# Two transformer blocks on one core: weight blocks in flight, the first modulation set in quarters, and a new written order

## The chip, the cores and the metric

The kernel runs on one core of a Trainium2 chip. The core has a matrix engine (TensorE, PE in the profile, with its weight loads as PEld), a vector engine (VectorE, DVE), a scalar engine (ScalarE, ACT), GpSimd (POOL) and SyncE (SP), which here issues nearly all transfers. The metric is device time in microseconds of the whole launch.

## The reference, cut to what matters

Two blocks work on 256 token rows of 1024 numbers (x) and on 256 context rows.

- **First block.** `mod = silu(c) @ w_mod + b_mod` gives six vectors for x; the same matrix with `c_ctx` gives those of the context. `h = rmsnorm(x) * n1 * (1 + scale) + shift`, and the like for the context. A gated linear attention follows: q, k, v, r are products of h with slices of `gla_w_in`, the decay comes from a small gate product, and `y = (norm(o) * silu(r)) @ w_out`; `x = x + g1 * y`. Then a mixture of 16 experts: each row is given two experts out of one of four groups, `out += gate * (silu(h@w1) * (h@w3)) @ w2`, `x = x + g2 * out`, and a last rmsnorm with `final_g`.
- **Second block.** Two layers of attention (latent and grouped heads; then windowed heads with a short convolution) on x, with keys and values of a second context that is projected from inputs of its own and does not depend on the first block.

Everything is in 32-bit floating point. The weights are read from HBM once: some 222 MB.

## The kernel before, in words

**How work is recorded and ordered.** The program is first recorded: every call on an engine becomes an `Op` (its function is called at line 384, which is therefore the line of almost all rows). `Sched.emit` (line 504) then plays the ops through a list planner with a cost for each op, picks an order, and issues the instructions in it. Each engine runs its own instructions strictly in that order, and SyncE issues the transfers strictly in that order too. An op's place is pulled forward or back by a table `PRI`: a number for its section (`sch.sec`, such as `rc2`, `rank`, `moe3`, `Gq`) and one for its run of 24 ops in the section.

**Buffers.** A weight block is mostly 1 MB (128 partitions of 8 KB). Blocks, split copies of weights (`cv`), projected heads and gathered rows share one pool `b` of 17 buffers of 8 KB a partition. Of these at most `WC = 5` may be weight blocks at a time (`sch.subcap`), and at most `CC = 5` split copies. PSUM has 8 banks (`ps`). A transfer into a buffer is issued when the last reader of the buffer's old content is done; until then SyncE stands, and all transfers behind it.

**The start** (line 1510). x is normed by rows. `gemv_half(h)` makes half of the first modulation set: four weight blocks (`modh`), on each of which 32-column products in four column groups run, then a copy by ScalarE, two transposes and six small VectorE ops. After both halves, section GN transposes x, modulates it (`split_evac`: a high and a low part), and section GM does so for the context. `dense` then makes q (`gq`), r (`gr0`, `gr1`) and k, v; the order of these sections is written in `GLASEQ`.

**The experts.** Routing is sections `rt`, `rc1`, `rc2`; section `rank` sorts the experts by their number of rows, and `eid` gives the expert number of each rank. Rank 15 is always expert 0. A load for another rank (`loadr`, line 2055) reads its expert number from `eid` into a register of SyncE (row line 2065), and its transfer's address is worked out from it (line 2066). So the first such load waits for `eid`. Each expert has six 1 MB blocks. The projections and attention of the second context (`cth`) are woven into the experts' sections by `merge` as other work for TensorE.

**Behind the experts.** `overflow` (line 2216) is an ordered stop of all engines: each reads a count and skips a branch that is not taken here (its rows have line 2222). Then section `t2` norms the result (`facc`) twice, as sums of squares over rows of 1024, and `adaln_T` (line 1218) transposes it for the second block.

Of the kernel before, what the change touches and what calls it, by code (L numbers as in the profile page):

```python
# [93 lines left out]
def _chunks(i):  # L94
# [10 lines left out]
    m = _kt(mods[0])[:, :, :2048].reshape(128, 8, 2, 2, 512)  # L105
    for h in range(2):
        for k2 in range(4):
            out[f"modh{h}_{k2}"] = m[:, 2 * k2:2 * k2 + 2, :, h]
# [43 lines left out]
def host(i):  # L152
# [40 lines left out]
ALT = 1  # L193
# [12 lines left out]
PRI = {  # L206
# [2107 lines left out]
```

## Time and profile before

| | |
|---|---|
| median of 3 runs | 891.46 us (890.01 to 892.35) |
| the profiled execution | 890.18 us, span 888.4 us |
| TensorE busy | 844.4 us (95%) |
| VectorE, ScalarE busy | 578.3 us, 416.4 us |
| mean granted TensorE clock | 0.991 |
| bytes read | 222 MB, mean 251 GB/s |

Busy time is the union of the recorded instructions. A matmul's record holds its latency, so that gaps shorter than it do not show as idle. PEld is the weight load of the matrix engine and overlaps PE. In the tables by stage PEclk is the granted clock as a share of full speed, "DMA share" the mean busy share of the 16 DMA engines.

### The profile page before, as it was taken

Reading aid. Unit: us, or ns where it says so; the run is one execution under the profiler, and the core shown is the slowest. Engines: PE = TensorE matmul, PEld = TensorE weight load, DVE = VectorE, ACT = ScalarE, POOL = GpSimd, SP = SyncE. Lnnn points to the kernel's source line nnn. Section 1 sums busy time; section 2 is a strip of 40 time slices with the busy share of each in tenths; the row PEclk is TensorE's granted clock in tenths of the full one; section 3 lists DMA queues with packets and bytes.
Section 4 is the critical chain, followed back from the end, with each engine's and each line's share of the span. In section 5 each row is a group of like instructions: output and inputs, shape, how many; then the busy total and the mean of one; then the engine's idle time right before and its main releaser. Section 6 shows DMA issues by size and latency. Waiting matters only on the chain. (4 is left out here: it accounts for less than half of the span.)

```text
span 888.4 us, 15257 instructions
## 1 busy us (share of the span) xinstructions
PE 844.4 (95%) x5830; PEld 598.1 (67%) x5830; DVE 578.3 (65%) x1608; ACT 416.4 (47%) x819; POOL 0.9 (0%) x5
## 2 busy tenths in 40 slices
PE   4999999999999999999988995999999999999997
PEld 2677667767875656555633432688876778899986
DVE  2676889428984623444755424989866558899783
ACT  3466545226433222224444433555489715454890
POOL 0000000000000000000000000000000000000000
PEclk9999999999999999999999999899999999999999
DMA  9954961877526999999999998884713203465101
GB/s 381 415 217 181 377 252 58 303 327 285 189 100 229 416 357 374 342 386 371 360 416 373 403 420 317 315 355 143 281 52 142 96 1 142 167 248 204 49 1 48
DMA packets 32834, 224.14 MB, mean 252 GB/s; under 512 B 3568, under 2 KB 3824, under 8 KB 7408
## 3 DMA queue, kind: packets, MB, share of 16 engines
q1 hardware_dynamic: 32608, 222.56, 64.6%
q8 instruction: 48, 0.79, 0.3%
q0 software_dynamic: 144, 0.52, 0.2%
q14 instruction: 34, 0.28, 0.1%
HBM read 222.02 MB, written 1.05 MB: 251 GB/s over the span
## 5 line engine op out<-in xcount | busy, mean ns | idle before, releaser
L384 DVE TENSOR_TENSOR cv<-w,cv 128x1024 fp32r<-128x1024 f32 (+3 forms) x128 | 145.2, 1150 | 26.5 <-ACT cv L384 26.3
L384 ACT ACTIVATE cv<-w 128x1024 fp32r<-128x1024 f32 (+3 forms) x128 | 124.3, 998 | 57.6 <-DMA w<-in_w_dram 36.5
L384 PE MATMUL ps<-hh,cv 128*128 128x256 f32 x576 | 114.4, 288 | 0.2 <-ACT cv L384 0.2
L384 PEld LDWEIGHTS ps<-hh,cv 128*128 128x128 f32 x576 | 92.2, 191 | 5.9 <-issue 4.1
L384 PE MATMUL ps<-w,xg 128*32 128x512 f32 (+1 forms) x544 | 87.8, 605 | 3.3 <-DMA w<-in_w_dram 3.2
L384 PE MATMUL ps<-hl,cv 128*128 128x256 f32 x288 | 81.4, 285 | 0.0
L384 PE MATMUL ps<-cv,hh 128*128 128x512 f32 (+2 forms) x288 | 78.5, 352 | 0.4 <-ACT hh L384 0.4
L384 ACT ACTIVATE t<-ps 128x512 f32<-128x512 f32 (+5 forms) x77 | 36.0, 477 | 84.1 <-PE ps L384 67.4
L384 PE MATMUL ps<-c_col,t 128*128 128x128 f32 x384 | 63.0, 280 | 5.6 <-ACT t L384 4.9
L384 PEld LDWEIGHTS ps<-c_col,t 128*128 128x128 f32 x384 | 44.1, 141 | 33.8 <-ACT t L384 22.0
L384 ACT ACTIVATE t<-ps,s,f 128x512 f32<-128x512 f32 (+1 forms) x80 | 54.9, 690 | 18.6 <-DVE s L384 18.3
L384 PE MATMUL ps<-w,cs 128*32 128x512 f32 (+1 forms) x448 | 50.9, 563 | 12.8 <-DVE s L384 9.1
L384 PE MATMUL ps<-cv,mixh 128*128 128x512 f32 x192 | 60.7, 394 | 0.0
L384 DVE TENSOR_REDUCE s<-ps 128x1 f32<-128x512 f32 (+1 forms) x80 | 45.1, 580 | 20.3 <-PE ps L384 20.1
L384 PE MATMUL ps<-w,t 128*32 128x512 f32 (+1 forms) x320 | 54.2, 599 | 3.6 <-issue 3.0
L384 PEld LDWEIGHTS ps<-hl,cv 128*128 128x128 f32 x288 | 54.9, 191 | 2.8 <-issue 2.4
L384 PEld LDWEIGHTS ps<-cv,hh 128*128 128x128 f32 x288 | 49.7, 189 | 10.0 <-issue 2.4
L384 PEld LDWEIGHTS ps<-w,xg 128*32 128x32 f32 (+1 forms) x544 | 23.0, 118 | 47.1 <-issue 37.0
L384 PE MATMUL ps<-cv,hl 128*128 128x512 f32 (+2 forms) x144 | 49.0, 348 | 0.0
L384 ACT ACTIVATE PT<-ps 128x512 f32<-128x512 f32 (+1 forms) x80 | 39.3, 510 | 20.6 <-PE ps L384 20.3
L384 PE MATMUL ps<-cv,hlh 128*128 128x512 f32 x128 | 42.1, 403 | 0.0
L384 PEld LDWEIGHTS ps<-cv,mixh 128*128 128x128 f32 x192 | 35.7, 188 | 7.3 <-issue 0.4
(269 smaller groups left out, 1515.5 us busy)
## 6 DMA issues: line engine op xcount, KB each, us to landing
w<-in_w_dram SPq DMA_DIRECT2D x198, 1024.0 KB, 7.5
ctx<-in_ctx_dram SPq DMA_DIRECT2D x3, 1024.0 KB, 7.8
w<-in_w_dram SPq DMA_DIRECT2D x4, 576.0 KB, 8.3
x<-in_x_dram SPq DMA_DIRECT2D x2, 1024.0 KB, 7.2
w<-in_w_dram SPq DMA_DIRECT2D x4, 512.0 KB, 3.7
w<-in_w_dram SPq DMA_DIRECT2D x2, 768.0 KB, 9.5
out_dram<-x SPq DMA_DIRECT2D x2, 512.0 KB, 2.6
c_cst<-in_cst_dram SPq DMA_DIRECT2D x1, 528.0 KB, 14.8
```

Source lines behind the costliest of these rows:

```text
L384: op.fn = lambda: getattr(real, fn)(*a, **k)
```

## The change

- **Weight blocks:** `WC` is 7, not 5. The pool `b` stays at 17 buffers.
- **First modulation set:** in four quarters, not two halves. A quarter takes two 1 MB blocks, 128-column products, one transpose, two VectorE ops. Behind each quarter stand a half block each (512 KB) of `gq` and `gr0`, two of eight column steps of x's transposing and modulating, and the products of `gq` and `gr0` on these two steps. Their sums stay in four PSUM banks from the first quarter to the last.
- **Products on zeros:** 20 of 512 columns at the start (section `wu`), and two of 256 columns behind each step of the first quarter, into a PSUM bank that nobody reads.
- **Experts' numbers:** the ops that make `eid` stand in a section of their own right behind the positions, ahead of the first gathering, not in `rank` behind it.
- **Norm behind the experts:** the products with `final_g` and the sums of squares by halves of 512 columns, and one add.
- **Order:** the planner runs four times, each time on the order of the run before and with a table of its own (364, 1462, 1331 and 1000 entries, not one of 356). The tables also name runs of six ops and single loads. From the third run on it takes each product as 1.5% longer, each transfer as 4.5% shorter and an issue as 2500 ns, not 1250. Section r is no longer woven with M in `GLASEQ`.

The core of the diff (the tables left out):

```diff
-    m = _kt(mods[0])[:, :, :2048].reshape(128, 8, 2, 2, 512)
-    for h in range(2):
-        for k2 in range(4):
-            out[f"modh{h}_{k2}"] = m[:, 2 * k2:2 * k2 + 2, :, h]
+    m = _kt(mods[0])[:, :, :2048].reshape(128, 8, 2, 4, 256)
+    for q in range(4):
+        for k4 in range(2):
+            out[f"modq{q}_{k4}"] = m[:, 4 * k4:4 * k4 + 4, :, q]
...
-WC = 5
+WC = 7
+OLDP = 2
...
-GLASEQ = "N q r+M k+l1 K v+L+2 R+3 f"
+GLASEQ = "N q r M k+l1 K v+L+2 R+3 f"
...
+        for n, pri in enumerate(PRIS):
+            if n == OLDP:
+                self.refine()
+            for op in self.main:
+                op.later = sum(pri.get(k, 0) for k in (op.grp, op.key, op.fine, op.ld))
+            order = self._pass(self.main)
+            self.main = [self.main[i] for i in order]
+        for op in self.main:
+            op.fn()
+
+    def refine(self):
+
+        self.ISSUE = dict(self.ISSUE, SP=2500.0, SD=2500.0)
+        for op in self.main:
+            op.cost *= 1.015 if op.eng == "PE" else 0.955 if op.eng == "SP" else 1.0
...
+    A1 = fix([8, 2], F32, "f")
+    zero = t2([512], F32R, "z")
+    V.tensor_scalar(zero, cs[0].rearrange("p a b -> p (a b)")[:, 0:1].to_broadcast([128, 512]), 0.0, None, op0=OP.mult)
+    idle = psum()
+
+    def busy(n, w):
+
+        for _ in range(n):
+            mm(idle[:, :w], zero[:, :128], zero[:, :w], True, True)
+
+    sch.sec = "wu"
+    busy(WARM, 512)
+    sch.sec = ""
+
+    def gemv_quarter(q):
 
         ps = psum()
-        for k2 in range(4):
-            w = load(f"modh{h}_{k2}")
-            for kt in (2 * k2, 2 * k2 + 1):
+        for k4 in range(2):
+            w = load(f"modq{q}_{k4}")
+            for k in range(4):
+                kt = 4 * k4 + k
                 with sch.together():
                     for g in range(4):
...
+                        o = k * 512 + g * 128
+                        mm(ps[32 * g:32 * g + 32, :128], cs[0][:, kt, :], w[:, o:o + 128], kt == 0, kt == 7)
+                    if q == 0:
+                        busy(2, 256)
+        r = t2([128])
+        S.activation(r, ps[:, :128], AF.Copy)
         pt = psum()
...
+        PE.transpose(pt[:, :128], r, ident)
+        o = modc[:, 0, 0].rearrange("p (a q j) v -> p a q j v", a=2, q=4)[:, :, q]
+        bias = col("bm0")[:, :16].rearrange("p (a q j) -> p a q j", a=2, q=4)[:, :, q]
+        V.tensor_tensor(o, pt[:, :128].rearrange("p (a j r) -> p a j r", a=2, j=2)[:, :, :, 0:2],
+                        bias[:, :, :, None].to_broadcast([128, 2, 2, 2]), op=OP.add)
+        c = slice(2 * q, 2 * q + 2)
+        V.scalar_tensor_tensor(A1[:, c, :], modc[:, 0, 0, 8 + 2 * q:10 + 2 * q, :], 1.0,
+                               col("n1")[:, c, None].to_broadcast([128, 2, 2]), op0=OP.add, op1=OP.mult)
...
+    early = {"gq": [Tjob(hl, pl)], "gr0": [tokjob(hl, t, pr[t]) for t in range(2)]}
+    blocks = {}
+    for q in range(4):
+        sch.sec = "G0"
+        gemv_quarter(q)
+        c2 = q % 2
+        for n in early:
+            off, ln = W["w"][f"{n}_{q // 2}"]
+            if not c2:
+                blocks[n] = b8([ln], n="w")
+            o_ = c2 * ln // 2
+            SY.dma_start(blocks[n][:, o_:o_ + ln // 2], bass.AP(
+                tensor=D["w"].tensor, offset=D["w"].offset + off + o_, ap=[[ln, 128], [1, ln // 2]]))
+        sch.sec = "GN"
+        trans_step(xl, modulated(hl, 0, 0), q)
+        for n, jobs in early.items():
+            sch.sec = "Gq" if n == "gq" else "Gr"
+            hi, lo = conv(blocks[n].rearrange("p (k n) -> p k n", n=512)[:, 2 * c2:2 * c2 + 2])
+            for k in range(2):
+                for j in jobs:
+                    j(2 * q + k, hi[:, k], lo[:, k], q + k == 0, 2 * q + k == 7)
+    bk("M")
+    norm_rows(xc, xc)
+    trans(xc, modulated(hc, 1, 256))
...
+    sch.sec = "eid"
...
+    eid = fix([16], I32, "f")
+    V.tensor_copy(eid, ef)
+    sch.sec = "rc2"
...
+    s4 = sm([2, 2, 2])
+    for t in range(2):
+        for half in range(2):
+            c = slice(half * 512, half * 512 + 512)
+            V.tensor_tensor(xn2[:, t, c], facc[:, t, c], fg[:, c], op=OP.mult)
+            sumsq(facc[:, t, c], 512, s4[:, half, 0, t:t + 1])
+            (sumsqv if t else sumsq)(xn2[:, t, c], 512, s4[:, half, 1, t:t + 1])
     ss = sm([2, 2])
-    for t in range(2):
-        V.tensor_tensor(xn2[:, t], facc[:, t], fg, op=OP.mult)
-        sumsq(facc[:, t], 1024, ss[:, 0, t:t + 1])
-        (sumsqv if t else sumsq)(xn2[:, t], 1024, ss[:, 1, t:t + 1])
+    V.tensor_tensor(ss, s4[:, 0], s4[:, 1], op=OP.add)
```

`trans_step(tiles, fn, k2)` is the body of the loop of `trans` (line 1003); `modulated` is the function `fn` that sections GN and GM had.

## Rows read from the trace of the kernel before

**Rows 1.** The page: busy time; busy share of the DMA engines by slices of 22.2 us
```profile
PE 844.4 (95%) x5830; PEld 598.1 (67%) x5830; DVE 578.3 (65%) x1608; ACT 416.4 (47%) x819; POOL 0.9 (0%) x5
...
DMA  9954961877526999999999998884713203465101
```

**Rows 2.** Busy time by stage: us, PE, PEld, DVE, ACT, POOL, PEclk, DMA share, GB/s
```profile
9.00:22.70 13.70, 10.78 (x90) 5.99 (x90) 2.95 (x16) 5.49 (x9) 0.00 (x0) 1.00 1.01 425
22.70:44.00 21.30, 20.98 (x163) 15.00 (x162) 14.11 (x32) 9.05 (x14) 0.00 (x0) 1.00 1.01 414
...
200.00:261.00 61.00, 59.78 (x333) 49.08 (x331) 53.20 (x161) 31.25 (x69) 0.00 (x0) 1.00 0.48 183
261.00:289.00 28.00, 28.00 (x160) 14.84 (x159) 14.70 (x59) 9.37 (x20) 0.00 (x0) 1.00 0.65 243
289.00:444.00 155.00, 153.85 (x996) 90.79 (x995) 73.91 (x195) 45.60 (x82) 0.00 (x0) 1.00 0.95 372
444.00:533.00 89.00, 77.83 (x522) 33.50 (x526) 39.24 (x141) 39.47 (x116) 0.00 (x0) 0.98 0.99 403
533.00:578.00 45.00, 34.71 (x199) 20.21 (x192) 32.58 (x85) 20.86 (x46) 0.00 (x0) 0.89 0.84 317
578.00:867.00 289.00, 286.73 (x2011) 244.26 (x2011) 229.41 (x690) 178.15 (x356) 0.00 (x0) 1.00 0.39 144
```

**Rows 3.** Timeline of TensorE, 9 to 23 us: start, us, what, idle before
```profile
9.08 1.93 PE L384 MATMUL ps<-w,cs 128*32 128x256 f32 x16 [9.08 <-DVE s L384]
...
12.30 3.46 PE L384 MATMUL ps<-c_col,x 128*128 128x128 f32 x15 [0.57 <-ACT x L384]
15.69 2.80 PE L384 MATMUL ps<-w,cs 128*32 128x256 f32 x48
18.99 0.44 PE L384 MATMUL ps<-c_col,t 128*128 128x128 f32 x2 [0.50 <-ACT t L384]
20.53 1.22 PE L384 MATMUL ps<-t,c_col 128*32 128x256 f32 x4 [1.11 <-DVE t L384]
...
22.72 0.50 PE L384 MATMUL ps<-hlh,cv 128*128 128x256 f32 x2
```

**Rows 4.** Timeline of the other engines in the same stretch
```profile
10.06 2.19 ACT L384 ACTIVATE x<-x,s 128x1024 f32<-128x1024 f32 x2 [2.43 <-DVE s L384]
...
18.55 0.38 ACT L384 ACTIVATE t<-ps 128x256 f32<-128x256 f32 x1 [6.31 <-PE ps L384]
...
19.46 0.37 DVE L384 TENSOR_TENSOR f<-ps,c_col 128x4 f32<-128x4 f32 x4 [9.51 <-PE ps L384]
```

**Rows 5.** Waits of SyncE's queue, 200 to 261 us: total, times, longest
```profile
SPq L384 <- PE ps L384: 42.9, 8, 13.2
SPq L2065 <- DVE t L384: 20.7, 1, 20.7
```

**Rows 6.** Waits of SyncE's queue, 289 to 444 us
```profile
SPq L2066 <- PE ps L384: 92.2, 36, 8.1
```

**Rows 7.** Waits of SyncE's queue, 444 to 533 us
```profile
SPq L2066 <- PE ps L384: 65.0, 25, 5.5
```

**Rows 8.** TensorE by form, 444 to 533 us: xcount, busy, mean ns, idle before
```profile
L384 PE MATMUL ps<-w,xg 128*32 128x512 f32 x188 | 28.2, 621 | 3.3 <-DMA w<-in_w_dram 3.2
```

**Rows 9.** Timeline of VectorE, 254 to 261 us
```profile
254.61 0.16 DVE L384 COPY s<-ps 128x16 f32<-128x16 f32 x1
...
257.44 1.22 DVE L384 TENSOR_TENSOR a<-f,t 128x1024 f32<-128x1024 f32 x1
...
258.90 1.21 DVE L384 TENSOR_REDUCE f<-a 128x64 f32<-128x1024 f32 x1
260.03 0.17 DVE L384 CAST f<-s 128x16 int32<-128x16 f32 x1
```

**Rows 10.** Waits of TensorE, 533 to 578 us
```profile
PE ps L384 <- PEq L2222: 3.7, 1, 3.7
...
PE ps L384 <- DVE xn L384: 2.0, 1, 2.0
```

More of the change, by code (lines that the diff above doesn't have):

```diff
@@ L279 @@
 XM = 0
+WARM = 20
 WPE = 0.0
@@ L297 @@
 CDSEQ = "kqc+x gB a+G o"
-GLASEQ = "N q r+M k+l1 K v+L+2 R+3 f"
+GLASEQ = "N q r M k+l1 K v+L+2 R+3 f"
 class Op:
-    __slots__ = ("eng", "fn", "acc", "cost", "lat", "preds", "npred", "succs", "tiles", "name", "later", "cols", "table", "grp", "tiled")
+    __slots__ = ("eng", "fn", "acc", "cost", "lat", "preds", "npred", "succs", "tiles", "name", "later", "cols", "table", "grp", "tiled", "key", "fine", "ld")
 class Sched:
@@ L502, in merge, with emit, _pass @@
         self.cur[i0:i1] = out
-    def emit(self, reorder=True, window=3000):
-        ops = self.main
+    def emit(self):
         seen = {}
-        for op in ops:
+        for op in self.main:
             k = seen[op.grp] = seen.get(op.grp, -1) + 1
-            op.later += PRI.get(op.grp, 0) + PRI.get((op.grp, k // 24), 0)
+            op.key, op.fine, op.ld = (op.grp, k // 24), (op.grp, -1 - k // 6), None
+            if op.eng == "SP":
+                k = seen["ld"] = seen.get("ld", -1) + 1
+                op.ld = "ld", k
+        for n, pri in enumerate(PRIS):
[9 more added lines that the diff above has]
+        self.ISSUE = dict(self.ISSUE, SP=2500.0, SD=2500.0)
+        for op in self.main:
+            op.cost *= 1.015 if op.eng == "PE" else 0.955 if op.eng == "SP" else 1.0
+    def _pass(self, ops, window=3000):
         hist = {}
@@ L529, in emit @@
                 (hw if wr else hr).append((i, r))
-        if not reorder:
-            for op in ops:
-                op.fn()
-            return
         n = len(ops)
@@ L700, in emit @@
         self.busy = {e: sum(o.cost for o in ops if o.eng == e) for e in engs}
-        self.order, self.st = order, st
-        self.ret = {}
-        for i in order:
-            self.ret[i] = ops[i].fn()
+        return order
 class Blocks:
@@ L902, in gemv_half @@
                 with sch.together():
                     for g in range(4):
-                        o = (kt % 2) * 1024 + g * 256
-                        mm(ps[32 * g:32 * g + 32, :256], cs[0][:, kt, :], w[:, o:o + 256], kt == 0, kt == 7)
-        r = t2([256])
-        S.activation(r, ps[:, :256], AF.Copy)
-        pt = psum()
-        for j in range(2):
-            PE.transpose(pt[:, j * 128:(j + 1) * 128], r[:, j * 128:(j + 1) * 128], ident)
-        o = modc[:, 0, 0].rearrange("p (a h g j) v -> p a h g j v", a=2, h=2, g=2)[:, :, h]
@@ L912, in gemv_half @@
-        bias = col("bm0")[:, :16].rearrange("p (a h g j) -> p a h g j", a=2, h=2, g=2)[:, :, h]
-        src = pt[:, :256].rearrange("p (j a g r) -> p a g j r", j=2, a=2, g=2)
-        for v in range(2):
-            for a in (1, 0):
-                V.tensor_tensor(o[:, a, :, :, v], src[:, a, :, :, v], bias[:, a], op=OP.add)
+                        o = k * 512 + g * 128
+                        mm(ps[32 * g:32 * g + 32, :128], cs[0][:, kt, :], w[:, o:o + 128], kt == 0, kt == 7)
+                    if q == 0:
+                        busy(2, 256)
@@ L1005, in trans, with trans_step @@
         for k2 in range(4):
-            ps = psum()
-            for j in range(2):
-                for i in range(2):
-                    kt = 2 * k2 + j
-                    PE.transpose(ps[:, j * 256 + i * 128:j * 256 + i * 128 + 128],
-                                 tiles[i][:, kt * 128:(kt + 1) * 128], ident)
-            for j in range(2):
-                fn(2 * k2 + j, ps[:, j * 256:(j + 1) * 256])
+            trans_step(tiles, fn, k2)
+    def trans_step(tiles, fn, k2):
+        ps = psum()
+        for j in range(2):
+            for i in range(2):
+                kt = 2 * k2 + j
+                PE.transpose(ps[:, j * 256 + i * 128:j * 256 + i * 128 + 128],
+                             tiles[i][:, kt * 128:(kt + 1) * 128], ident)
+        for j in range(2):
+            fn(2 * k2 + j, ps[:, j * 256:(j + 1) * 256])
     def conv(src, tag="c"):
@@ L1510, in _build @@
     norm_rows(xl, xl)
-    AB_ = [(fix([8], F32, "f"), modv(0, 0, v)) for v in range(2)]
-    wq = []
-    for h in range(2):
-        gemv_half(h)
-        for v in range(2):
-            c = slice(4 * h, 4 * h + 4)
-            V.scalar_tensor_tensor(AB_[v][0][:, c], modv(0, 1, v)[:, c], 1.0, col("n1")[:, c], op0=OP.add, op1=OP.mult)
-        wq.append(load(f"gq_{h}"))
-    (Al, Bl), (Ac, Bc) = AB_
+    sch.sec = "GM"
     xc = rows2("ctx", SY)
@@ L1522, in _build, with modulated @@
     wga = col("wga").rearrange("p (k n) -> p k n", k=8)
-    lps = pd()
     bk = Blocks(sch, "G")
-    for (name, h, x_, A, B, o) in (("N", hl, xl, Al, Bl, 0), ("M", hc, xc, Ac, Bc, 256)):
-        bk(name)
-        if h is hc:
-            norm_rows(xc, xc)
+    bk("N")
+    lps, pl, pr = pd(), [pd(), pd()], [pd(), pd()]
+    def modulated(h, v, o):
         def fn(kt, ps):
             f = t2([256])
-            split_evac(ps, h.hi(kt), h.lo(kt), A[:, kt:kt + 1], B[:, kt:kt + 1], f, ALT and kt % 2)
+            split_evac(ps, h.hi(kt), h.lo(kt), A1[:, kt, v:v + 1], modv(0, 0, v)[:, kt:kt + 1], f, ALT and kt % 2)
             g = kt % 4
             mm(lps[32 * g:32 * g + 32, o:o + 256], wga[:, kt, :], f, kt < 4, kt >= 4)
-        trans(x_, fn)
+        return fn
+    early = {"gq": [Tjob(hl, pl)], "gr0": [tokjob(hl, t, pr[t]) for t in range(2)]}
[22 more added lines that the diff above has]
+    trans(xc, modulated(hc, 1, 256))
     low = t2([512], F32R), t2([512], F32R)
@@ L1562, in _build @@
     kT, qT = kq[:, 0], kq[:, 1]
-    pl = [pd(), pd()]
-    dense("gq", 512, [Tjob(hl, pl)], pre=wq)
     for i in range(2):
@@ L1570, in rproj @@
     def rproj(rh):
-        pss = [pd(), pd()]
-        dense(f"gr{rh}", 512, [tokjob(hl, 0, pss[0]), tokjob(hl, 1, pss[1])])
+        pss = [pd(), pd()] if rh else pr
+        if rh:
+            dense("gr1", 512, [tokjob(hl, 0, pss[0]), tokjob(hl, 1, pss[1])])
         for t in range(2):
@@ L1873, in _build @@
     iota = C("iota")
+    sch.sec = "eid"
+    iota = C("iota")
+    cnt_ = sm([16])
+    V.tensor_copy(cnt_, pps[:, 32:48])
+    key = sm([16])
+    V.scalar_tensor_tensor(key, cnt_, 16.0, iota[:, 0:16], op0=OP.mult, op1=OP.subtract)
+    V.memset(key[:, 0:1], -1e6)
+    big = t2([16, 16])
+    V.tensor_tensor(big, key[:, None, :].to_broadcast([128, 16, 16]), key[:, :, None].to_broadcast([128, 16, 16]), op=OP.is_gt)
+    rank = sm([16])
+    V.tensor_reduce(rank, big, axis=AX.X, op=OP.add)
+    perm = t2([16, 16])
+    V.tensor_tensor(perm, rank[:, None, :].to_broadcast([128, 16, 16]), iota[:, 0:16, None].to_broadcast([128, 16, 16]), op=OP.is_equal)
+    big = t2([16, 16])
+    V.tensor_tensor(big, perm, iota[:, None, 0:16].to_broadcast([128, 16, 16]), op=OP.mult)
+    ef = sm([16])
+    V.tensor_reduce(ef, big, axis=AX.X, op=OP.add)
+    eid = fix([16], I32, "f")
+    V.tensor_copy(eid, ef)
+    sch.sec = "rc2"
     oh = b8([2, NSLOT], F32R, "oh")
```

49 lines of the change are left out of this document (27 added, 22 removed), and 746 rows, old and new, of tables (PRI, PRIS).

## The prediction

> **What bounds the kernel now.** I read the page first: TensorE is busy 844.4 of 888.4 us [rows 1], so only 44 us can be won without making its work cheaper, and the question is where they lie. The table by stage [rows 2] answers it. From 578 to 867 us TensorE idles 289 - 286.7 = 2.3 us: nothing to win there, and much to lose if a new order puts a wait in. From 22.7 to 44 us it idles 0.3 us, from 200 to 261 us 1.2, from 261 to 444 us 1.2. Most of the idle time stands in three places: 9 us before the first product plus 2.9 us up to 22.7 us (11.9 together), 11.2 us from 444 to 533 us, and 10.3 us from 533 to 578 us. The granted clock is below 1 in the last two (0.98 and 0.89), which costs 0.02 x 77.8 = 1.6 and 0.11 x 34.7 = 3.8 us of busy time.
>
> Each place has its own limit. At the start TensorE waits for the first modulation blocks, which come one behind another: DMA share 1.01, 425 GB/s, so 2.47 us for a block of 1.049 MB [rows 2]. The first is used at 9.08 us, the fourth can be there at 16.5, the half's products end at 18.49 and the first wide product on the modulated rows starts at 22.72 [rows 3].
>
> From 444 to 533 us the DMA share is 0.99: the experts' weights set the time, and TensorE waits. But the stage before it, 289 to 444, is the other way round: TensorE is full (153.9 of 155), the DMA share is 0.95 at 372 GB/s, and SyncE's queue stood 92.2 us, in 36 waits, for products to give their blocks back [rows 6]. And before that DMA engines idled for long: share 0.48 from 200 to 261 us and 0.65 to 289 us [rows 2], 32 and 10 us of them. There SyncE stood 42.9 us for blocks in use and 20.7 us once for the experts' numbers [rows 5]. So transfers wait for TensorE first and TensorE for transfers later, with the same five blocks between them. That is what the profile says of this kernel; the rest of the change has to be measured against it.
>
> From 533 to 578 us a chain of single waits sets the time: the last expert's results, the stop of all engines (3.7 us) and the norm (2.0 us until its first transposes) [rows 10].
>
> **The first set by quarters.** A quarter's products need two blocks, there at 9.08 + 2.47 = 11.55 us; before, a half's fourth came at 16.5. After them: a step of 256 columns in four groups is 8 instructions at 2.80 / 48 = 58 ns = 0.47 us [rows 3]; with 128 columns I bound it by half and the whole, and take 0.27 us. Four steps after the second block: 1.1 us. Before, 4.23 us pass from the end of the half's products (18.49) to the first wide product (22.72): copy 0.38 us, transposes 0.44, VectorE 0.37 for four, then modulation and split [rows 3, 4]. One transpose and two VectorE ops in place of two and six save some 0.6: 3.6 us. x is normed at 12.25 us [rows 4], in time. So the first wide product starts at 11.55 + 1.1 + 3.6 = 16.25, 6.5 us earlier.
>
> Not all of this is won, since TensorE has by then done less. Of a half's products (64 x 58 ns = 3.7 us) it did a quarter's, 8 x 0.27 = 2.2: it owes 1.5 us. Of the sixteen transposes perhaps four are done; twelve cost at most 12 x 0.23 = 2.8 by the slow row (3.46 us for 15) and half that by the pace of the later ones: 1.4. Of the gate products' 1.85 us (20.53 to 22.72 without the wait) half: 0.9. And four quarters take 8.8 us of products against 7.4 for two halves: 1.4. Sum 5.2, net gain 1.3 us. The bounds are the whole 6.5 us and a loss of 3 (the owed work in the way, and each quarter's chain of 3.6 us open). The chain is covered by the quarter's wide products: 24 of 256 and 12 of 512 columns, at the row's 250 ns for 256 [rows 3] at most 12 us, while a quarter's 3 MB come in 7.4 us. So TensorE, not the transfers, should be the limit from 16 us on. The smaller pieces of `gq` and `gr0` move the same bytes; I cost them at nothing, and if each of the 8 cost one more 0.3 us issue behind a full queue it is hidden under that cover.
>
> **The zeros.** The half's first 16 instructions took 1.93 us, 121 ns each, those from 15.69 us on 58 ns [rows 3]; the clock column shows 1.00 there [rows 2], but the pace says that TensorE ran at the lower of its two levels (1.2, not 2.4 GHz) until then, after 9 us without work. Products on zeros before 9 us lift this: 16 x 63 ns = 1.0 us, and 1.7 us of the transposes, where they are on the path. They can also be in the way: 20 of 512 columns are at most 20 x 0.5 us by the row of 22.72 us, at half pace 20 us, at least 5. From some 1.5 us on they end between 6.5 and 21 us; I take 10, under the wait for the second block. Gain 0.7 us, bounds +2.7 and -9.
>
> **Seven blocks.** No work is removed; two more transfers may run ahead. What it can be worth: from 289 to 533 us come 155 x 0.372 + 89 x 0.403 = 93.5 MB; at 425 GB/s that is 220 us, not 244, and two blocks fetched in the idle stretches before 289 us save 4.9 more. Together 29 us at most by the transfers. TensorE caps this: it idles 1.2 us from 289 to 444, 11.2 to 533, and loses 1.6 to the clock; the 10.3 us behind 533 are mostly the serial chain. The lower bound is zero: the pool stays at 17, so a weight block more is another buffer less. Between 0 and 14 I take 10, nearer to the upper end, because the waits for blocks in use are long in every stage (42.9, 92.2 and 65.0 us [rows 5 to 7]) while the gap that they leave at TensorE is small. The products on expert weights idle only 3.3 us directly for a transfer there [rows 8]; the rest of the 11.2 waits on work that hangs on them.
>
> The row of 9 to 22.7 us shows 425 GB/s, and 403 stand over 89 us. The Trainium skill, "DMA: Bandwidth & Descriptors", Specifications, puts the share of one core in the HBM at about 358 GB/s. By that the 372 GB/s of 289 to 444 us would be the ceiling already and this term zero, 10 us less gain; the trace does not agree.
>
> **Experts' numbers early.** From the copy of the counts (254.61) to the cast (260.03) VectorE also runs ops of the later part: 1.22 and 1.21 us [rows 9]. Moved behind the cast, they free SyncE 2.4 us sooner from its 20.7 us wait, with DMA engines idle. What waits behind that load on SyncE are all later transfers; TensorE is full there, so it counts only through the stock. I take 1.5 us, bounds 0 and 2.4.
>
> **Norm by halves.** The first transposes wait 2.0 us for two whole rows' product [rows 10]; by halves the first four column steps are free after three pieces of four. I take 0.5 us; the sums take more and smaller instructions on both engines, with nothing behind the stop of engines to cover them, hence bounds of +1 and -1.
>
> **Order.** Everything is placed anew, also in 578 to 867 us. Idle there is 2.3 us and elsewhere some 3; the transfers behind the experts and the 3.8 us of lower clock from 533 to 578 can be won in part if more side work is left for that gap. I take 4, bounds +8 and -8.
>
> **Sum.** 1.3 + 0.7 + 10 + 1.5 + 0.5 + 4 = 18 us. The profiled execution took 890.2, the median is 891.5, so 890.2 - 18 = 872.2, set against the median 873.5. I predict 873 us.
>
> **Rivals.**
> - *The stages balance fully.* Seven blocks carry the whole 14 us, order 8, the start 4: 28 or more, 850 to 862. For it: both limits are in sight of each other in 289 to 533 us. Against: the stop of engines stays. 0.14.
> - *The blocks change nothing.* The pool of 17, not the five, ends SyncE's waits, or the weights come no faster than now; then start, numbers, norm and order alone give 4 to 8 us: 884 to 888. For it: the same 17 buffers hold the context's work too. The rule of the Trainium skill cited above ("DMA: Bandwidth & Descriptors", Specifications) gives this case. Against: 0.48 DMA share with SyncE at a stand. 0.13.
> - *Within 0.3%* (2.7 us, about what a measurement of this kernel tells from no change): gains eaten by one new wait. 0.05.
> - *Slower: weight blocks drive out the side work.* Two more of 17 buffers go to weights, the context's attention runs later, and its products fall behind the experts instead of into the gap. From 444 to 533 us TensorE is busy 77.8 us, of which 28.2 with the 32-column products on experts' first weights [rows 8] and a part with their second; perhaps 25 us are side work. If 60% of it, 15 us, move behind 533 us, the sum turns by 15 and 10 gained are lost: 890.2 + 15 - 8 = 897. It decides from some 18 us moved on without a gain of the blocks, or 10 with none of order. For it: the same pool. Against: transfers wait in every stage, side work nowhere visibly. 0.09.
>
> The forecast keeps 0.59, its own range 863 to 883. Faster 0.86, same 0.05, slower 0.09. The range that leaves out 2 in 10 runs from 855, inside the first rival, to 888, the upper end of the second.
>
> **What the profile after would show.** Right: wide products from 16 to 17 us on, pace of the first products 58 ns; DMA share above 0.6 between 200 and 261 us and near 1 from 265 us on; the experts' last transfer 8 to 15 us earlier; idle from 444 to 533 us under 4 us; 578 to 867 us as long as now for the same work. Wrong would be: SyncE's waits for blocks as long as before with the DMA share at 0.95 (second rival), context products behind the stop of engines (fourth), or idle time of TensorE of over 5 us in its last 290 us.

## The result

The changed kernel takes 901.62 us, median of 4 runs (900.61 to 904.48); the kernel before took 891.90 on the same chip (890.01 to 892.47). The ratio is 1.0104, 95% interval 1.0066 to 1.0142: slower by 1.0%, where 2% faster was forecast. The profiled execution took 902.59 us with a span of 900.8, against 888.4: 12.4 us more. The medians lie 9.7 us apart: the profiled execution before took 1.7 us less than its median, the one after 1.0 us more, and what the two traces account for is the 12.4 us.

The page of the changed kernel, busy time of each engine:
```profile
PE 856.0 (95%) x5994; PEld 604.2 (67%) x5994; DVE 583.1 (65%) x1610; ACT 417.4 (46%) x827; POOL 0.8 (0%) x5
```
TensorE is busy 11.6 us longer than in [rows 1] and idles as long (44.8 us). The table by stage, columns as in [rows 2]:
```profile
9.00:22.70 13.70, 11.21 (x101) 7.48 (x99) 3.38 (x9) 4.30 (x4) 0.00 (x0) 0.88 1.00 390
22.70:44.00 21.30, 20.91 (x290) 17.00 (x286) 11.45 (x23) 8.40 (x14) 0.00 (x0) 1.00 1.02 412
200.00:261.00 61.00, 60.42 (x338) 49.06 (x337) 50.76 (x145) 30.55 (x54) 0.00 (x0) 1.00 0.58 225
261.00:289.00 28.00, 27.50 (x157) 14.85 (x156) 16.88 (x68) 7.60 (x19) 0.00 (x0) 1.00 0.55 212
289.00:444.00 155.00, 152.64 (x966) 85.34 (x963) 72.63 (x170) 45.08 (x79) 0.00 (x0) 1.00 0.92 357
444.00:533.00 89.00, 79.36 (x542) 38.57 (x544) 47.74 (x178) 44.96 (x129) 0.00 (x0) 0.98 0.99 394
533.00:578.00 45.00, 28.88 (x176) 10.67 (x168) 20.33 (x50) 15.19 (x35) 0.00 (x0) 0.92 0.89 361
578.00:867.00 289.00, 286.97 (x1995) 243.82 (x1994) 226.58 (x702) 171.78 (x354) 0.00 (x0) 1.00 0.40 151
```
What to see: the DMA engines do less, not more, where blocks were to run ahead (261 to 289 us: 0.55 against 0.65; 289 to 444: 357 GB/s against 372). From 444 to 533 us TensorE still idles 9.6 us. From 578 us on TensorE is as full as before.

Times of single steps are compared best as a chain of five stretches, read from both timelines: the experts' numbers reach SyncE at 265.6 us instead of 260.2 (+5.4); from the first expert block's issue (1.0 us behind the numbers) to the landing of the 26th block 99.0 us instead of 94.0 (+5.0); from there to the landing of the last, the 90th, 186.2 instead of 186.6 (-0.4); from that to the end 349.0 instead of 346.6 (+2.4, of which 1.5 until the first piece is normed and 0 from there to the first wide product, 9.1 in both). Sum: 12.4.

The start, timeline of TensorE of the changed kernel, to be laid beside [rows 3]:
```profile
4.93 4.44 PE L1046 MATMUL ps<-z 128*128 128x512 f32 x11 [4.93 <-DVE z L1046]
11.37 0.55 PE L1046 MATMUL ps<-c_col,x 128*128 128x128 f32 x3 [1.99 <-ACT x L1046]
12.41 2.18 PE L1046 MATMUL ps<-c_col,x 128*128 128x128 f32 x9 [0.49 <-ACT x L1046]
14.24 2.83 PE L1046 MATMUL ps<-z 128*128 128x512 f32 x9
17.00 0.43 PE L1046 MATMUL ps<-w,cs 128*32 128x128 f32 x8
17.36 0.51 PE L1046 MATMUL ps<-z 128*128 128x256 f32 x2
17.79 0.43 PE L1046 MATMUL ps<-w,cs 128*32 128x128 f32 x8
...
22.53 0.43 PE L1046 MATMUL ps<-w,cs 128*32 128x128 f32 x8
22.88 0.51 PE L1046 MATMUL ps<-z 128*128 128x256 f32 x2
...
27.17 1.19 PE L1046 MATMUL ps<-cv,hlh 128*128 128x512 f32 x4
```
The first quarter's two blocks landed at 9.04 and 11.53 us, but its products (`w,cs`) begin at 17.00, behind twelve transposes of x and all 20 products on zeros (`z`), and behind each step of eight stand two more zeros: 0.79 us a step, 6.0 us for the eight steps, so that ScalarE's copy starts at 23.02. The first wide product stands at 27.17 us instead of 22.72. The first eleven zeros did not lift the clock for the transposes behind them: they ended at 9.37 us, TensorE then waited 1.99 us for x, the granted clock was 0.65 from 11.0 to 14.2 us, and twelve transposes took 0.55 + 2.18 us, as much each as the fifteen of [rows 3].

VectorE of the changed kernel at the experts' numbers, for [rows 9]:
```profile
261.00 0.17 DVE L1046 COPY s<-ps 128x16 f32<-128x16 f32 x1 [1.08 <-PE ps L1046]
...
265.40 0.17 DVE L1046 CAST f<-s 128x16 int32<-128x16 f32 x1
...
265.56 1.22 DVE L1046 TENSOR_TENSOR a<-f,t 128x1024 f32<-128x1024 f32 x1
```
From copy to cast 4.4 us, 5.4 before. The operation of 1.22 us now stands behind the cast, as meant.

Waits of SyncE's queue, 200 to 261 us, for [rows 5], 289 to 444 us, for [rows 6] (L2777 is the line that issues an expert block), and 444 to 533 us, for [rows 7]:
```profile
SPq L1046 <- PE ps L1046: 24.6, 5, 8.4
SPq L1046 <- DVE cv L1046: 13.7, 3, 7.7
```
```profile
SPq L2777 <- PE ps L1046: 90.1, 32, 6.4
```
```profile
SPq L2777 <- PE ps L1046: 65.6, 30, 5.3
```
Ahead of the numbers the queue stands 38.3 us for products and conversions instead of 44.9 (42.9 in [rows 5] and 2.0 for VectorE's conversions), and 13.7 of the 38.3 are for conversions. In the experts' stage the waits for products were 92.2 and 65.0 us before: with up to seven blocks the queue stands as long as with five. The expert products of 32 columns wait for transfers as before, for [rows 8]:
```profile
L1046 PE MATMUL ps<-w,xg 128*32 128x512 f32 x164 | 24.6, 626 | 3.3 <-DMA w<-in_w_dram 3.1 <-ACT t L1046 0.2
```
And TensorE's waits from 533 to 578 us, for [rows 10], where the halves were to help:
```profile
PE ps L1046 <- DVE xn L1046: 6.5, 1, 6.5
PE ps L1046 <- DMA w<-in_w_dram: 5.7, 5, 2.0
```
The 6.5 us hold the stop of engines and the norm in one; before, the two were 3.7 and 2.0 us, with eight products between them. There is less other work in this stretch (TensorE busy 28.9 us against 34.7), and the transfers, 10 us late, are waited for here too.

### The profile page after: what moved, and what is told of

Read it like the earlier page. It is cut to its first block, busy times and chain, and to the rows that moved or that the text cites. A ratio compares the mean times of both kernels' runs of the same rounds, so it can differ in the third digit from the quotient of the medians.

```text
span 900.8 us, 15630 instructions
## 1 busy us (share of the span) xinstructions
PE 856.0 (95%) x5994; PEld 604.2 (67%) x5994; DVE 583.1 (65%) x1610; ACT 417.4 (46%) x827; POOL 0.8 (0%) x5
## 5 line engine op out<-in xcount | busy, mean ns | idle before, releaser
L1046 PEld LDWEIGHTS ps<-hh,cv 128*128 128x128 f32 x576 | 92.2, 190 | 10.0 <-issue 6.6
L1046 ACT ACTIVATE t<-ps,s,f 128x512 f32<-128x512 f32 (+1 forms) x80 | 55.3, 698 | 13.0 <-DVE s L1046 11.6
L1046 PEld LDWEIGHTS ps<-cv,hh 128*128 128x128 f32 x288 | 49.8, 189 | 10.3 <-ACT hh L1046 1.8
L1046 PE MATMUL ps<-cv,hlh 128*128 128x512 f32 x128 | 44.1, 413 | 0.0
## 6 DMA issues: line engine op xcount, KB each, us to landing
w<-in_w_dram SPq DMA_DIRECT2D x4, 576.0 KB, 10.3
```

The source lines that it names most:

```text
L1046: op.fn = lambda: getattr(real, fn)(*a, **k)
```

## The experiments

Each planner's order was written out as a list and replayed, so that one part can change and all else stand. `old` and `new` are the orders of the two kernels, each operation named by its counterpart in the other program; one whose input is not made yet stands behind what makes it. The edit to replay:
```diff
-        for n, pri in enumerate(PRIS):
...
-            self.main = [self.main[i] for i in order]
+        self.main = [self.main[i] for i in ORDER]
         for op in self.main:
             op.fn()
```
The kernel before stood at 892.0 to 892.7 us beside each group of runs. A ratio is that to the kernel before on the same chip, over all runs, and so can differ by 0.2% from that of the medians. The stretches are those of the profiled execution of each run, one trace for each: those of f1, k2 and f5 took 902.4, 900.5 and 900.1 us, 3 to 8 us over the median. The first weight block alone landed up to 2.2 us later than in the trace of before (g2; f2 and f5 1.3), which shifts the column of the numbers.

| run | us | ratio (95%) | numbers at | to 26th block | to 90th | to the end |
|---|---|---|---|---|---|---|
| before | 892 | 1 | 260.2 | 94.0 | 186.6 | 346.6 |
| changed | 901.6 | 1.0104 (1.0066 to 1.0142) | 265.6 | 99.0 | 186.2 | 349.0 |
| e1_silent | 900.1 | 1.0090 (1.0065 to 1.0115) | 265.4 | 99.0 | 186.9 | 349.4 |
| e2_quarter_first | 900.5 | 1.0098 (1.0081 to 1.0116) | 263.7 | 99.3 | 184.1 | 347.0 |
| f2_front | 897.0 | 1.0059 (1.0033 to 1.0086) | 264.6 | 94.3 | 185.2 | 348.0 |
| e4_old_all | 898.6 | 1.0067 (1.0052 to 1.0083) | 267.9 | 94.5 | 186.6 | 347.4 |
| e3_old_from_eid | 900.2 | 1.0086 (1.0058 to 1.0113) | 265.8 | 95.6 | 188.9 | 347.8 |
| f1_old_start | 899.3 | 1.0059 (1.0036 to 1.0081) | 262.9 | 99.2 | 188.2 | 349.2 |
| g1_new_from_eid | 900.1 | 1.0075 (1.0049 to 1.0100) | 260.6 | 100.0 | 186.4 | 348.5 |
| g2_new_to_eid | 895.9 | 1.0031 (1.0006 to 1.0055) | 264.9 | 96.0 | 185.9 | 348.7 |
| k1_new_from_25 | 897.8 | 1.0056 (1.0033 to 1.0080) | 260.2 | 96.0 | 189.7 | 350.8 |
| k2_new_to_25 | 897.3 | 1.0051 (1.0029 to 1.0072) | 261.5 | 104.6 | 184.6 | 347.1 |
| f4_hoist | 896.3 | 1.0038 (1.0016 to 1.0060) | 261.2 | 92.9 | 188.7 | 350.7 |
| e5_before_seven | 901.6 | 1.0097 (1.0062 to 1.0132) | 262.7 | 94.5 | 191.1 | 348.4 |
| f3_numbers | 902.2 | 1.0094 (1.0060 to 1.0128) | 258.0 | 106.8 | 186.0 | 347.8 |
| f5_two_behind | 891.8 | 0.9981 (0.9957 to 1.0005) | 260.6 | 101.7 | 187.9 | 347.0 |
| k3_halves | 893.5 | 1.0013 (0.9997 to 1.0029) | 260.1 | 94.5 | 186.6 | 347.5 |

**The start.** `e1_silent`: the zeros left out.
```diff
             mm(idle[:, :w], zero[:, :128], zero[:, :w], True, True)
+            sch.cur[-1].fn = lambda: None
```


> The changed kernel in its own order, with the 36 products on zeros (20 of 512 columns, 16 of 256) left out; nothing of the result hangs on them. Theory A, the zeros stand in the way: they took 7.5 + 3.5 us of TensorE, in part while it would have waited; the first wide product comes 5 to 7 us before 27.2 us, and the time is 894 to 897 instead of 901.6. Theory B, they only fill time in which TensorE waits for x, or the lower clock without them costs what they cost: the first wide product at 26 to 27 us, and the time 900 to 903.


Measured: 900.1 us. The first wide product comes at 22.9 us, 4.3 us earlier and so nearly as theory A had it (5 to 7), and yet the numbers only 0.2 us earlier. Table by stage of this run, 9 to 44 us:
```profile
9.00:22.70 13.70, 9.29 (x149) 7.32 (x149) 5.10 (x13) 5.44 (x7) 0.00 (x0) 1.00 1.01 393
22.70:44.00 21.30, 18.69 (x215) 15.44 (x211) 9.43 (x17) 7.37 (x11) 0.00 (x0) 0.92 1.01 412
```
Without them TensorE idles 2.6 us from 22.7 to 44 us, the clock is 0.92 there, and the modulation products up to the numbers take 12.4 us in sum instead of 9.8. The 11 us of zeros stood where TensorE would have waited or run slowly: they earn what they take. The time is that of theory B.

`e2_quarter_first`: the same with the first quarter moved ahead.
```diff
-ORDER = new
+ORDER = new[:40] + quarter0_products + x_transposes[:4] + quarter0_copy_and_modulation + rest_of_new
```


> As the kernel without the products on zeros, and with the first quarter's products, their copy, its transposes and its modulation moved ahead of every other instruction of their engines at the start (of the conversions for gq and gr0, and of x's other transposes). Theory A, what stands ahead of the first quarter costs the rest of the start: the first wide product at 17 to 20 us, and 889 to 893. Theory B, the owed work only comes later, so that TensorE has the same work ahead of 44 us: the first wide product earlier but the time within 2 us of the kernel that only leaves the zeros out.


Measured: 900.5 us, first wide product at 23.1. The move came out by half only: the products write the bank of the zeros, could not be put ahead of their (now empty) places in the list, and twelve transposes still ran first; the products began at 15.0 us.

`f2_front`: a start by hand, in which that is mended, with the old order behind it.
```diff
-ORDER = new
+start = zeros[:8] + block0_products + x_transposes[:4] + block1_products + quarter0_copy_and_modulation
+ORDER = start + [i for i in new[:590] if i not in start]
+ORDER += [i for i in old if i not in ORDER]
```


> The changed kernel with a start set by hand: 8 of the 36 products on zeros (those that end before the first block), then the first quarter's products as each block lands, between them the transposes of x, then its copy and modulation; the half block that only the third quarter needs is issued behind the second quarter's blocks; behind the start the order of the kernel before, as in the run that keeps the changed start (898.6 us). Theory A, the quarters were spoilt only by what stood ahead of them: the first wide product at 17 to 19 us, experts' numbers by 262 us, and 890 to 894. Theory B, TensorE has the same work to do before the numbers and idled only 2 us there, so quarters can win nothing: first wide product at 17 to 20 us, and 894 to 898.


Measured: 897.0 us, first wide product at 23.6 us, numbers at 264.6. In this profiled execution the first block landed at 10.2 us, 1.3 later than in the one of before; the rest of the 4.4 us is not that. The time is that of theory B; the wide product came later than both theories had it. TensorE in this run:
```profile
10.26 1.08 PE L601 MATMUL ps<-w,cs 128*32 128x128 f32 x32 [1.84 <-DMA w<-in_w_dram]
...
14.03 1.38 PE L601 MATMUL ps<-w,cs 128*32 128x128 f32 x32
...
23.59 1.19 PE L601 MATMUL ps<-cv,hlh 128*128 128x512 f32 x4
```
The first quarter's products now follow their blocks, and still 8.2 us pass from their end to the first wide product, where 3.6 was forecast: the granted clock is 0.50 from 16 to 19 us, and the rest of x's transposes and the second quarter's products stand between.

`e4_old_all`: the changed start as it is, the old order behind it.
```diff
-ORDER = new
+ORDER = new[:590] + [i for i in old if i not in new[:590]]
```


> The changed kernel with the order of its start (to some 30 us) kept, and the order of the kernel before behind it, the experts' numbers in their old place too. Theory A, start and order make the whole loss: the start's 4.4 us stay, 894 to 897. If the numbers' new place is worth the 1.0 us that they took less, it is 1 us above the kernel that keeps the new order up to them. Theory B, the loss at the start is made up or doubled later, whatever the order: 891 to 893, or over 899.


Measured: 898.6 us, between the two. The changed start costs 6.0 us (898.6 - 892.6; this kernel keeps the norm by halves, see `k3_halves`); a new order behind it only some 3 more.

**The order.** `f1_old_start`: the old start, the new order and its blocks behind it.
```diff
-ORDER = old
+ORDER = old[:444] + [i for i in new if i not in old[:444]]
```


> The kernel before (halves, no products on zeros, the norm by whole rows) with its own start, and behind it the instructions in the order of the changed kernel, which sets up to seven weight blocks ahead and the experts' numbers early. Theory A, the start makes the loss of some 6 us and the new order the rest of 3: 894 to 897. Theory B, the start makes all of it and order and blocks are worth nothing: 891 to 893. Theory C, order and blocks gain what was predicted, hidden by a start that costs twice as much: 880 to 886.


Measured: 899.3 us, above all three. So order and blocks lose 6.6 us by themselves, as much as the start.

`e3_old_from_eid` and `g1_new_from_eid` change the order at the experts' numbers, `g2_new_to_eid` ahead of them:
```diff
-ORDER = new
+ORDER = new[:1790] + [i for i in old if i not in new[:1790]]
```
```diff
-ORDER = old
+ORDER = old[:1737] + [i for i in new if i not in old[:1737]]
```
```diff
-ORDER = old
+ORDER = f1_order[:1751] + [i for i in old if i not in f1_order[:1751]]
```


> The changed kernel in its own order up to the experts' numbers (some 265 us), and in the order of the kernel before from there on; the work is the same. Theory A, the new order behind the numbers loses the 5.7 us by which the experts' weights fall back between 270 and 390 us: 895 to 897, and the last transfer of the experts lands some 5 us before 551.8. Theory B, the fall back comes from the state in which the new start and the seven blocks leave the buffers at 265 us: 900 to 903.

> The kernel before in its own order until the experts' numbers are made, and in the order of the changed kernel from there on (weight blocks up to seven ahead where that order has them). With the old start and the new order throughout it was 899.3. Theory A, the part behind the numbers loses: the numbers stay at 260 us, from the experts' first transfer to the landing of the last pass 283 to 287 us in place of 280.6, and 896 to 899. Theory B, the loss is made ahead of the numbers: 891 to 894.

> The other half: the kernel before with its own start, the order of the changed kernel until the experts' numbers are made (at 263 us in place of 260), and its own order from there on. Theory A, each half loses its own part: 894 to 896, with the 280 us of the old order behind the numbers. Theory B, all of it is lost ahead of the numbers, in the state of the buffers: 897 to 900. Theory C, nothing is lost here: 891 to 893.


Measured: 900.2, 900.1 and 895.9 us. With the new order behind the numbers it is 8.2 us slower than before, with the new order ahead of them 3.9, and both together (f1) no more than the larger one. So theory A of `g2_new_to_eid` holds in its number, that of `g1_new_from_eid` in its mechanism with a longer time than expected (the 286.4 us from the first issue to the last landing lie inside its 283 to 287, the 900.1 us above its 899). With the changed start, going back to the old order at the numbers won 1.4 us at most, inside the spread (theory B of that run).

`k1_new_from_25` and `k2_new_to_25` cut the stretch behind the numbers once more, at the 26th block, where each run with the new order had lost its 5 us:
```diff
-ORDER = old
+ORDER = old[:2318] + [i for i in new if i not in old[:2318]]
```
```diff
-ORDER = old
+ORDER = g1_order[:2337] + [i for i in old if i not in g1_order[:2337]]
```


> The kernel before in its own order up to the transfer of the experts' 26th weight block (some 95 us behind the first), and in the order of the changed kernel from there on. Theory A, the new order loses its 5 us ahead of this point, where in each trace with it the blocks 20 to 25 take 19 us in place of 15: the 25th lands as before, the last within 1 us of before, and 892 to 894.5. Theory B, it loses all the way: 896 to 900.

> The other piece: the order of the changed kernel only between the experts' numbers and the 26th block's transfer, the order of the kernel before ahead of it and behind it. Theory A, the loss lies here: the 25th block lands 94 to 95 us behind the first issue in place of 94.0 - 5 = 89, and 896 to 899. Theory B, it lies behind: 891.5 to 894.


Measured: 897.8 and 897.3 us: 5.5 and 5.0 us. My theory that the loss lies ahead of the 26th block has fallen; each half loses most of the whole. In k2 a part of the 104.6 us is the clock, which falls to 0.66 from 262 to 270 us. In k1 the later blocks take 189.7 us and the rest 350.8.

**Seven blocks.** `f4_hoist`: the kernel before, each weight transfer put as early in the list as 17 buffers and seven blocks allow (55 places on the mean), no engine's own sequence changed.
```diff
-ORDER = old
+ORDER = old with each weight transfer moved ahead while weight_blocks <= 7 and buffers <= 17
```


> The kernel before with each weight block's transfer put as early in the order as the 17 buffers allow, up to seven at a time in place of five; the order on every engine's own queue stays as it was, only the buffers that the transfers are given come free earlier. Theory A, the sum of the prediction: the stock in the experts' stage makes the last transfer land 5 to 10 us sooner, DMA share over 0.6 from 200 to 261 us, and 882 to 888. Theory B, the pool is full where it matters and TensorE's order gives buffers back no sooner: 891 to 893. Theory C, a block taken early holds a buffer that other work then waits for: over 894.


Measured: 896.3 us, theory C. Waits of SyncE's queue in this run, 289 to 444 us (L2082 issues the expert blocks), and three rows of its table by stage:
```profile
SPq L2082 <- PE ps L597: 74.1, 32, 8.1
SPq L597 <- PE ps L597: 18.4, 7, 5.3
SPq L2082 <- DVE cv L597: 18.0, 4, 10.3
```
```profile
200.00:261.00 61.00, 59.60 (x332) 49.31 (x332) 52.55 (x159) 31.22 (x66) 0.00 (x0) 1.00 0.48 183
289.00:444.00 155.00, 153.02 (x989) 89.23 (x985) 71.86 (x177) 44.27 (x78) 0.00 (x0) 1.00 0.92 372
444.00:533.00 89.00, 79.15 (x528) 35.28 (x527) 41.56 (x160) 41.15 (x119) 0.00 (x0) 0.96 1.00 406
```
Blocks do run ahead: the wait for products falls from 92.2 to 74.1 us and the 26th lands 1.1 us sooner behind the first issue. But the queue now waits 18.0 us for VectorE's conversions (4.8 before), 10.3 of them in one piece; ahead of the numbers the DMA share stays at 0.48, and from 289 to 444 us the rate at 372 GB/s, both as in [rows 2]; and the last block lands 2.0 us later than before. The run hoists transfers in the whole program, not only the experts': of the 6.1 us by which its span is longer, 2.8 lie behind the first wide product of the second block (327.1 us from there to the end, 324.3 before). So 3.6 us is the price of this hoisting; for the experts' stage alone it says that seven blocks win nothing.

`e5_before_seven`: the kernel before, placed anew by its planner with one number changed.
```diff
-WC = 5
+WC = 7
```


> The kernel before with one number changed, seven weight blocks at a time in place of five, so that its planner places everything anew with the same priorities; nothing else of the change. Theory A, blocks ahead are the gain that was predicted: 880 to 886. Theory B, blocks ahead are worth nothing, and an order that was not picked by its time loses by being another: 895 to 905.


Measured: 901.6 us, theory B, as slow as the whole change. That it is the other order which costs, and not the blocks, is likely by the replays but not separated in this run.

**The numbers.** `f3_numbers`: the chain together, ahead of all else on VectorE.
```diff
-ORDER = old
+ORDER = old with the nine operations of the numbers' chain in one piece, from the counts' copy on
```


> The kernel before in its own order with one edit: VectorE's chain for the experts' numbers stands together, ahead of the other work that was mixed into it. Theory A, the queue is freed 1.0 us sooner and the stock of transfers grows by as much: 890.5 to 892, or 0.5 to 1.5 us under the kernel before. Theory B, the order of give-back by TensorE sets the transfers, and the chain is worth nothing: within 0.5 us.


Measured: 902.2 us, 9.4 slower, which neither theory had, though the cast stands at 257.86 us, 2.2 sooner. VectorE, and TensorE's waits from 250 to 295 us, in this run:
```profile
257.86 0.17 DVE L597 CAST f<-s 128x16 int32<-128x16 f32 x1
257.94 0.17 DVE L597 TENSOR_SCALAR f<-f 128x32 f32<-128x32 f32 x1
258.15 0.36 DVE L597 TENSOR_TENSOR oh<-c_cst,f 128x64 fp32r<-128x64 f32 x2
```
```profile
PE ps L597 <- DVE oh L597: 2.4, 1, 2.4
```
TensorE waits for the selection matrices (`oh`), which now stand behind the chain. The wait is 2.4 us; what follows is the dear part, in its table by stage:
```profile
258.00:262.00 4.00, 3.48 (x21) 3.39 (x23) 2.93 (x7) 2.30 (x9) 0.00 (x0) 0.69 0.44 145
262.00:266.00 4.00, 4.00 (x15) 2.33 (x15) 0.65 (x2) 0.99 (x3) 0.00 (x0) 0.50 0.30 121
266.00:270.00 4.00, 4.00 (x12) 1.23 (x9) 3.38 (x24) 0.99 (x4) 0.00 (x0) 0.50 0.27 59
270.00:274.00 4.00, 4.00 (x17) 2.63 (x15) 0.98 (x3) 1.79 (x4) 0.00 (x0) 0.50 0.48 203
274.00:278.00 4.00, 4.00 (x16) 1.65 (x14) 1.65 (x7) 0.32 (x1) 0.00 (x0) 0.67 0.49 131
```
The granted clock is 0.50, 1.2 GHz, until some 276 us: four products of 512 columns take 1.98 us there (first line) and 1.08 in the kernel before (second line).
```profile
261.75 1.98 PE L597 MATMUL ps<-w,t 128*64 128x512 f32 x4
261.50 1.08 PE L384 MATMUL ps<-w,t 128*64 128x512 f32 x4
```
The 26th block lands 106.8 us behind the first issue instead of 94.0.

`f5_two_behind`: only the two operations of 1.2 us put behind the cast, `oh` left ahead.
```diff
-ORDER = old
+ORDER = old with a<-f,t and the reduction f<-a moved behind the cast of the numbers
```


> The kernel before in its own order with only VectorE's two operations of 1.2 us on 1024 columns put behind the cast of the experts' numbers; what TensorE waits for there (its selection matrices) stays ahead, which it did not in the run with the whole chain together (902.2 us, TensorE waited 2.4 us and its granted clock fell to 0.50 for some 17 us). Theory A, that wait and the clock were the whole loss there, and an earlier number is worth what it is early: cast 1.2 to 2.4 us sooner, clock 1.00 from 254 to 289 us, and 890 to 892. Theory B, the sooner number is worth nothing, since TensorE gives the blocks back no sooner: 892 to 893.5. Theory C, any move at this place costs: over 895.


Measured: 891.8 us; the interval allows 0.43% faster and 0.05% slower. That is the upper end of theory A, 0.2 us from the range of theory B; the run can't tell the two apart. Its profile is of an execution of 900.1 us. The chain from copy to cast took 3.4 us there (257.02 to 260.40) instead of 5.4, but all of it came later (its first block landed 1.3 us later than in the trace of before), so that the cast was not sooner than the 260.03 us of before; no profile shows an execution near the median. And the clock, against theory A, falls once more:
```profile
258.00:260.00 2.00, 2.00 (x20) 1.90 (x18) 1.68 (x6) 1.36 (x6) 0.00 (x0) 1.00 0.00 0
260.00:262.00 2.00, 2.00 (x12) 1.15 (x12) 1.93 (x4) 1.18 (x6) 0.00 (x0) 0.89 0.04 8
262.00:270.00 8.00, 8.00 (x28) 4.65 (x28) 5.17 (x28) 2.61 (x8) 0.00 (x0) 0.50 0.73 262
```

**The norm.** `k3_halves`: the kernel before with the norm by halves.
```diff
-        V.tensor_tensor(xn2[:, t], facc[:, t], fg, op=OP.mult)
-        sumsq(facc[:, t], 1024, ss[:, 0, t:t + 1])
+        for half in range(2):
+            c = slice(half * 512, half * 512 + 512)
+            V.tensor_tensor(xn2[:, t, c], facc[:, t, c], fg[:, c], op=OP.mult)
+            sumsq(facc[:, t, c], 512, s4[:, half, 0, t:t + 1])
...
+    V.tensor_tensor(ss, s4[:, 0], s4[:, 1], op=OP.add)
```


> The kernel before in its own order with the norm behind the experts by halves, and nothing else of the change. Theory A, as the two traces show it (9.1 us from the first normed piece to the first wide product in both): within 0.5 us of the kernel before, 891.5 to 893. Theory B, the halves put more and smaller instructions on the chain behind the stop of engines: 893 to 894.


Measured: 893.5 us, 1.1 above the kernel before; the interval reaches from 0.3 us faster to 2.6 slower.

No version beats the kernel before by more than a measurement can tell; f5 comes nearest.

## Why the prediction was wrong

The terms added up to 18 us won; 9.7 us were lost. The terms that failed are the seven blocks (+10, nothing won), the order (+4, 6.6 to 8.2 us lost) and the start (+1.3, 6.0 lost).

**Start: +1.3 forecast, a loss of 6.0 measured** (e4, zeros and norm by halves included). The step that failed is the first wide product at 16.25 us, from which the net gain was taken. It came at 27.17 us: the quarter's products did not start as their blocks landed (9.04 and 11.53 us), but at 17.00, behind twelve transposes and the zeros. Nor was there much to win. Adding up TensorE from its first product to the numbers, in times from one product's start to the next, with what exceeds 0.7 us counted as idle: before 249.1 us of work, 2.0 idle, 9.1 until the first product. That left quarters some 2 us to win, however early the first wide product came. In the run with the zeros out the wide product is as early as before (22.9 against 22.7 us), yet the numbers are 5.2 us late: the twelve transposes and then the first products begin at 11.2 instead of 9.1 us, work is 251.4 and idle 2.8. The quarters' products cost 0.3 us more than the halves' (9.8 us against 9.5), where 1.4 was forecast.

**Zeros: +0.7 forecast, bounds +2.7 and -9.** The 20 of 512 columns were to end at 10 us; eleven did, and nine stood between the transposes and the first quarter, not "under the wait for the second block". They took 7.5 us. The 16 of 256 columns inside the first quarter, 3.5 us, had no price in the sum at all. By e1 they are worth about nothing either way (901.6 against 900.1 us, intervals that overlap).

**Seven blocks: +10 forecast, -3.6 measured** (f4), and -9.7 with the planner's new placing (e5). This was the largest term and the failed one. I read SyncE's 92 us of waiting as a want of blocks. What the runs show is that more blocks ahead move no more bytes. The account that fits is TensorE's pace: while it is full, from 261 to 444 us, blocks come free at the rate of its products, whatever their number. That is argued, not shown: the pool of 17 stayed in every run, so a pool that is full, the condition of my second rival, was not told apart from it. I had written that TensorE is full there, and still took a value near the upper end. At 70 us behind the first issue 18 blocks had landed in the kernel before, in the changed one and in f4 alike. The share of 0.58 from 200 to 261 us, close to the 0.6 that I had named as a sign of success, was only the 0.59 (before 0.74) of 150 to 200 us made good: (225 - 183) x 61 and (284 - 233) x 50 are 2.6 MB each.

The rival that the blocks change nothing was right about the blocks, and wrong to let the other terms stand. In the rows of f4, 444 to 533 us, the weights come at 406 GB/s. The share of some 358 GB/s that the Trainium skill gives one core ("DMA: Bandwidth & Descriptors", Specifications) was no ceiling here.

**Numbers early: +1.5 forecast.** The chain itself took 1.0 us less in the changed kernel and 2.0 less in f5; the time of f5 moved by no more than the measurement is uncertain. A wait that it can cause was not in my bounds: in f3 the same step, done too far, cost 9.4 us.

**Norm by halves: +0.5 forecast with bounds of 1; -1.1 measured**, not told from zero (k3).

**Order: +4 forecast, bounds +8 and -8; 6.6 (f1) and 8.2 us (g1) lost.** The step that failed is to take a new placing as a gain; the measured loss lies at the lower bound. The order of the kernel before seems to fit as a whole: pieces of the new one, placed in it, lose 3.9 (g2), 5.0 (k2) and 5.5 us (k1), and the losses don't add up: k1 and k2 together are g1 and cost 8.2, start (6.0) and order (6.6) together 9.7. What in a piece costs most was not settled. In k1 the clock stays at 1.00 from 261 to 444 us, and the loss is spread over the later blocks and 533 to 578 us, where the clock is 0.81 and TensorE busy 29.9 of 45 us.

**The rival that came out slower** (897 us, 0.09) was the right side by another way. No side work fell behind the experts: behind the last block's landing TensorE has 2,228 products to run, before 2,232, and from 533 to 578 us it does less (28.9 against 34.7 us).

**What was right:** the reading of where the 44 us of idle time lie, the stretch from 578 us on, and that 444 to 533 us is set by the experts' weights, whose share stays 0.99.

## What to carry to other kernels

Before you give a queue that waits for buffers more of them, look whether the engine that gives them back is idle; in this kernel it was full, its pace was the better guess, and two more blocks were worth nothing. An earlier first result is worth no more than the idle time that lies between it and the next point where all work meets. When a planner places everything anew, write its order out and replay it: then each part can be priced alone, and the price of the order itself is seen.

## What the runs showed of the hardware

The granted clock of TensorE fell to 0.50 behind the experts' numbers, for 17 us in f3, 10 in f5 and some 7 in k2. In f3 it fell behind a wait of 2.4 us. The Trainium skill ("TensorE: Matmul & The Clock Gate", Why this matters for your kernels) warns of idle gaps between bursts of products, which bring the low clock back; f3 agrees in kind, though its gap is shorter than the one named there. In f5 there was no such gap: TensorE was, by its records, busy in all of 254 to 262 us, with gather products of 64 columns (0.28 us each) and four of 512, and the clock fell at 261.5 us all the same, while the same products in the kernel before kept 1.00 in its profile. So idle gaps explain the first case at most; what tips the second is open, and whether the runs of the kernel before that lie some 4 to 7 us over its median (10 of the 60 beside f1 and f5) have the same reason was not shown.

The first block of weights landed between 8.7 (f3) and 11.1 us (g2) in executions of programs with the same first transfers, and a DMA share of 0.99 from 444 to 533 us stood for 394 GB/s in the changed kernel and 406 in f3: a full share is not one rate.
